# An encoder on one core: gather rows beside the projections paced at 0.42 and not 0.7, and taken in turn with leftover routing in the experts' pass

## The chip, the cores and the metric

The kernel runs on one core of one Trainium2 chip. The metric is the device time of one execution in microseconds (us), and the median over several executions counts. One execution was also profiled; every view below comes from it. PE is TensorE (matmuls), PEld its weight loads, DVE is VectorE, ACT is ScalarE, POOL is GpSimd, and SP is SyncE, which here only issues DMAs.

## The reference, cut to what matters

An encoder layer runs on two requests of 256 and 1024 tokens (ten tiles of 128 tokens) of width 1024. First come a mixer (retention and latent attention) and a cross attention over memory tokens. The last step, where most of the time goes, is a layer of 16384 single-neuron experts, of which each token uses 128:

```python
q = (xt @ wq).reshape(PEER_BLOCK, PEER_HEADS, PEER_QUERY_DIM)
s1 = jnp.einsum('thd,hkd->thk', q[..., :half], sub_keys[0])
s2 = jnp.einsum('thd,hkd->thk', q[..., half:], sub_keys[1])
v1, i1 = lax.top_k(s1, PEER_TOPK)
v2, i2 = lax.top_k(s2, PEER_TOPK)
...
ts, sel = lax.top_k(cand, PEER_TOPK)
ids = jnp.take_along_axis(cidx, sel, axis=-1).reshape(PEER_BLOCK, PEER_HEADS * PEER_TOPK)
g = jax.nn.softmax(ts.astype(jnp.float32), axis=-1).reshape(PEER_BLOCK, PEER_HEADS * PEER_TOPK)
a = jnp.einsum('td,ted->te', xt, U[ids]).astype(jnp.float32)
w = (g * jax.nn.gelu(a, approximate=False)).astype(xt.dtype)
return jnp.einsum('te,ted->td', w, V[ids])
```

Choosing the 128 experts of each token (the two lists of 16, their 16 best pairs, the ids and the weights g) is called routing below.

## The kernel before, in words

Matrix products are in float32, each made of three passes over split operands (`mm3`, L170: high times high, high times low, low times high).

The program has these stages. `phase_a` computes the retention. `phase_b` over block 0 (tiles 0 and 1) comes next, then `phase_m` for the second request (its latent attention, head pair by head pair), then `phase_b` over block 1 (tiles 2 to 5) and block 2 (tiles 6 to 9). A block in `phase_b` is a chain of projections: the output projection `w_out` with a residual add (`ld<-pj,ld`) and a norm, `ca_wq`, the cross attention, `ca_wo` with a residual add and a norm, and `peer_wq` with the key scores. Then `gates` (L1067) writes a table of gates, and `dense` (L1147) is the experts' pass.

The experts are computed in two ways. Six tiles (2 to 7) go through `dense`: for all 128 blocks of 128 experts, in 43 groups of three blocks (the last has two), PE computes the products with U (`pa`), ACT and DVE make the gated weights (`wr`, `wl`), and PE multiplies these with V (`pv`); DVE adds each result to the tile's sum (`dacc<-pv,dacc`, six per group). POOL makes the low halves of the weights U and V (`ul`, L1175, and `vl`, L1199). The other four tiles (0, 1, 8, 9: `GATHER`) fetch only the experts that their tokens chose. For each of the 128 experts of a token, a gather row is one indirect DMA on POOL's queue (128 rows of 4 KB, one for each token, into a tile `grow`) and one DVE instruction over 128x1024: 128 rows of U (`gj<-grow,...`, a dot product) and then 128 rows of V (a multiply-add into a sum). Four tiles make 1024 gather rows.

Where a gather row finds its second operand depends on when it starts. `banks` (L1046) copies x or the sum into PSUM (`gps`) if the pool `gps` exists, which is opened just ahead of `dense` (L1265). Before that the operand stands in SBUF (`gx`, `gacc`). The tiles `grow` rotate over four slots; `gx` and `gacc` join them when a tile starts after `gps` is open, and three more when all routing is done.

Routing and gather rows are generators in two queues, `self.routing` and `self.gathering`. They are laid beside the projections by a pace: as the program is written out, every matmul group calls `tick(us)` with its estimated time, `tick` adds `us * rho` to a debt, and `step` writes pieces of one queue until the debt is paid (a gather row counts 1.2). `RHO` (L50) has a pair for each stage, the first number for as long as routing waits in its queue, the second when only rows do: `phase_m` and `phase_b` of blocks 1 and 2, then `gates`, then `dense`. `step` takes routing first and rows only when no routing is left. What is left when `dense` has been written out is written behind it. A scheduler then puts each engine's instructions into a fixed order; each engine runs its own in that order and waits where an operand is late.

Of the kernel before, what the change touches and what calls it, by code (L numbers as in the profile page):

```python
# [46 lines left out]
NG = 3  # L47
O1_BY = "va"

RHO = ((0.75, 0.7), (0.5, 0.0), (0.9, 0.55))  # L50
LATE = 2

MORE = 3
# [10 lines left out]
class Lead:  # L64


    def __init__(self, k):
        self.k = k
# [39 lines left out]
class K:  # L108
    def __init__(self, nc, tc, I, O, dbg=None):
        self.nc, self.tc, self.I, self.O = nc, tc, I, O  # L110
        self.dbg = dbg or {}
        self.n = 0
        self.routing, self.gathering = [], []
        self.keeps = []
        self.spare = ()
        self.routed = set()
        self.owed, self.rho = 0.0, (0.0, 0.0)
        self.gps = self.rp = None
        self.slots, self.at = ["grow"] * 4, 0
        self.anchor = None  # L120
        self.v, self.vf = Lead(self), Fill(self)

    def tick(self, us):


        rho = self.rho[0 if self.routing else 1]
        if self.rho is RHO[1] and self.routed.issuperset(DENSE):
            rho = 0.0
# [5 lines left out]
            self.owed -= self.step()  # L134

    def step(self, q=None):
        q = q or self.routing or self.gathering
        try:
            return next(q[0])
        except StopIteration:  # L140
            q.pop(0)
            if self.gps is not None and not self.routing and self.rp is not None:

                self.rp.release()
                self.rp = None
                self.more = self.tc.alloc_tile_pool(name="more", bufs=1, side="right", reuse_waits="tile")
                self.slots += ["more"] * MORE
            return 0.0
# [1083 lines left out]
    def run(self):  # L1232
        nc, tc, I = self.nc, self.tc, self.I
        with ExitStack() as es:
# [21 lines left out]
            self.phase_b(sd, BLOCKS[:1], lambda: self.phase_m(sd, 0, self.lw))  # L1256
            self.rho = RHO[0]
            self.phase_m(sd, 1, self.lw)
            self.mw.release()
            self.phase_b(sd, BLOCKS[1:])  # L1260
            self.rho = RHO[1]
            self.dense_inputs(es.enter_context(tc.tile_pool(name="dx", bufs=1, reuse_waits="tile")))
            self.gates(sd)
            self.rho = RHO[2]
            self.gps = es.enter_context(tc.tile_pool(name="gps", bufs=1, reuse_waits="tile", space=PSUM))  # L1265
# [81 lines left out]
```

## Time and profile before

| | |
|---|---|
| median of three runs | 4372.47 us (4365.78 to 4373.7) |
| profiled execution, its own time | 4367.04 us |
| its span, first to last instruction | 4365.2 us |
| busy share of the span: PE, DVE, POOL, ACT | 92%, 75%, 53%, 38% |
| mean granted TensorE clock | 0.967 of full speed |

A busy PE is one with matmuls in its pipeline, and not a PE at its peak. What counts is which wait ends last in a stage, so the stages are read one by one: `phase_m` for the second request to about 1114 us, block 1 to 1490, block 2 to 1822, `gates` to 2111, `dense` to the end. Granted clock 1.00 is 2.4 GHz; a half-speed stretch is 1.2 GHz.

### The profile page before, as it was taken

Reading aid. Unit: us, or ns where it says so; the run is one execution under the profiler, and the core shown is the slowest. Engines: PE = TensorE matmul, PEld = TensorE weight load, DVE = VectorE, ACT = ScalarE, POOL = GpSimd, SP = SyncE. Lnnn points to the kernel's source line nnn. Section 1 sums busy time; section 2 is a strip of 40 time slices with the busy share of each in tenths; the row PEclk is TensorE's granted clock in tenths of the full one; section 3 lists DMA queues with packets and bytes.
Section 4 is the critical chain, followed back from the end, with each engine's and each line's share of the span. In section 5 each row is a group of like instructions: output and inputs, shape, how many; then the busy total and the mean of one; then the engine's idle time right before and its main releaser. Section 6 shows DMA issues by size and latency. Waiting matters only on the chain.

```text
span 4365.2 us, 66436 instructions
## 1 busy us (share of the span) xinstructions
PE 4010.5 (92%) x23202; PEld 3578.9 (82%) x23202; DVE 3281.7 (75%) x7044; ACT 1639.9 (38%) x3569; POOL 2301.6 (53%) x2090
## 2 busy tenths in 40 slices
PE   7999988899788988887798999999999999999999
PEld 7999877666587877876787888888988889888888
DVE  5556422798576799699788878888887888878883
ACT  6333535455343243498522222222222223222223
POOL 2221244013667710277537776666777677766662
PEclk9999999899899989999999999999999999999999
DMA  2112578237789866577648988888888889888882
GB/s 89 37 40 71 202 240 286 80 103 223 261 271 334 278 227 228 186 219 211 212 127 295 325 302 297 311 294 299 310 307 301 285 300 328 316 298 295 289 286 85
DMA packets 489008, 1030.74 MB, mean 236 GB/s; under 512 B 42720, under 2 KB 201952, under 8 KB 488672
## 3 DMA queue, kind: packets, MB, share of 16 engines
q0 software_dynamic: 149536, 545.33, 35.5%
q1 hardware_dynamic: 329200, 470.66, 32.6%
q10 hardware_dynamic: 9936, 10.51, 0.8%
q8 instruction: 182, 2.98, 0.3%
q14 instruction: 154, 1.26, 0.1%
HBM read 901.87 MB, written 124.45 MB: 235 GB/s over the span
## 4 chain that ended last, share of the span: by engine, by line
PE 26%; issue 8%; POOL 6%; DVE 6%; DMA 3%; ACT 1%; SPq 0%; POOLq 0%; ACTq 0%; DVEq 0%
PE pa L175 5%; PE pa L173 5%; PE pa L174 5%; PE pv L174 4%; PE pv L173 4%; PE pv L175 4%; POOL grow L1025 4%; DMA ur<-in_uT 2%; POOL vl L1199 1%; POOL ul L1175 1%; DVE gps L90 1%; DVE wr L74 1%; DVE dacc L74 1%; DVE wl L74 1%; DVE gj L90 1%
## 5 line engine op out<-in xcount | busy, mean ns | idle before, releaser
L1025 POOL DMA_INDIRECT grow<-in_peer_u,gids x512 | 537.1, 1049 | 533.9 <-DVE gj L90 213.0
L1025 POOL DMA_INDIRECT grow<-in_peer_v,gids x512 | 522.5, 1020 | 545.5 <-DVE gps L90 159.9
L173 PE MATMUL pa<-dxT,uh 128*128 128x384 f32 x2048 | 689.0, 337 | 17.4 <-ACT wr L1186 15.0
L174 PE MATMUL pa<-dxT,uh 128*128 128x384 f32 x2048 | 688.6, 336 | 0.0
L175 PE MATMUL pa<-dxT,ul 128*128 128x384 f32 x2048 | 676.4, 337 | 9.3 <-POOL ul L1175 9.3
L173 PE MATMUL pv<-vh,wh 128*128 128x512 f32 x1536 | 603.7, 397 | 40.1 <-DVE dacc L74 40.1
L174 PE MATMUL pv<-vl,wh 128*128 128x512 f32 x1536 | 609.7, 397 | 12.4 <-POOL vl L1199 11.7
L175 PE MATMUL pv<-vh,wl 128*128 128x512 f32 x1536 | 608.9, 396 | 1.4 <-DVE wl L74 1.4
L90 DVE SCALAR_TENSOR_TENSOR gps<-grow,ga,gps 128x1024 f32<-128x1024 f32 x384 | 493.2, 1284 | 9.6 <-ACT gps L1052 2.9
L90 DVE SCALAR_TENSOR_TENSOR gj<-grow,gps 128x1024 bf16<-128x1024 f32 x384 | 466.7, 1215 | 11.2 <-DMA grow<-in_peer_u,gids 3.1
L206 POOL TENSOR_TENSOR wl<-wraw,wh 128x512 fp32r<-128x512 f32 x180 | 250.7, 1409 | 310.7 <-ACT wh L202 241.2
L173 PEld LDWEIGHTS pa<-dxT,uh 128*128 128x128 f32 x2048 | 386.4, 189 | 31.7 <-ACT wr L1186 16.5
L1199 POOL TENSOR_TENSOR vl<-vr,vh 128x512 fp32r<-128x512 f32 x256 | 331.2, 1313 | 146.4 <-ACT vh L1198 144.3
L175 PEld LDWEIGHTS pa<-dxT,ul 128*128 128x128 f32 x2048 | 385.2, 189 | 21.2 <-POOL ul L1175 15.6
L1175 POOL TENSOR_TENSOR ul<-ur,uh 128x512 fp32r<-128x512 f32 x256 | 337.3, 1321 | 106.8 <-ACT uh L1174 103.5
L74 DVE TENSOR_TENSOR dacc<-pv,dacc 128x1024 f32<-128x1024 f32 x258 | 311.8, 1218 | 108.1 <-PE pv L175 107.6
L174 PEld LDWEIGHTS pa<-dxT,uh 128*128 128x128 f32 x2048 | 386.3, 189 | 6.3
L173 PEld LDWEIGHTS pv<-vh,wh 128*128 128x128 f32 x1536 | 292.7, 191 | 104.6 <-DVE dacc L74 48.5
L1174 ACT CAST uh<-ur 128x512 fp32r<-128x512 f32 x256 | 158.3, 621 | 553.4 <-DMA ur<-in_uT 510.2
L74 DVE TENSOR_TENSOR wr<-wr,gt 128x384 f32<-128x384 f32 x256 | 196.2, 767 | 209.2 <-ACT wr L1186 184.2
L174 PEld LDWEIGHTS pv<-vl,wh 128*128 128x128 f32 x1536 | 293.2, 191 | 73.2 <-POOL vl L1199 18.4
L175 PEld LDWEIGHTS pv<-vh,wl 128*128 128x128 f32 x1536 | 292.9, 191 | 58.4 <-DVE wl L74 1.8
(287 smaller groups left out, 9373.8 us busy)
## 6 DMA issues: line engine op xcount, KB each, us to landing
ur<-in_uT SPq DMA_DIRECT2D x256, 256.0 KB, 4.1
vr<-in_peer_v SPq DMA_DIRECT2D x256, 256.0 KB, 4.0
G<-st SPq DMA_DIRECT2D x96, 512.0 KB, 6.2
gt<-G SPq DMA_DIRECT2D x64, 768.0 KB, 7.2
wraw<-in_peer_wq SPq DMA_DIRECT2D x96, 256.0 KB, 5.9
wraw<-in_w_out SPq DMA_DIRECT2D x48, 256.0 KB, 5.1
wraw<-in_ca_wq SPq DMA_DIRECT2D x48, 256.0 KB, 3.6
x<-ld SPq DMA_DIRECT2D x24, 512.0 KB, 6.6
```

The costliest lines, as they stand in the source:

```text
L74: r = f(*a, **kw)
L90: r = f(*a, **kw)
L173: mm(ps, a[0], b[0], start=first, stop=False)
L174: mm(ps, a[0], b[1], start=False, stop=False)
L175: mm(ps, a[1], b[0], start=False, stop=last)
L206: (nc.vector if self.spare and k in self.spare else eng).tensor_tensor(wl[:, :n], raw[:, :n], r32(wh[:, :n]), ALU.subtract)
L1025: nc.gpsimd.indirect_dma_start(out=u, out_offset=None, in_=src, in_offset=bass.IndirectOffsetOnAxis(ap=ids[:, s:s + 1], axis=0))
L1174: nc.scalar.copy(uh, ur)
L1175: nc.gpsimd.tensor_tensor(ul, ur, r32(uh), ALU.subtract)
L1199: nc.gpsimd.tensor_tensor(vl, vr, r32(vh), ALU.subtract)
```

## The change

Two edits. The pace of gather rows beside `phase_m` and the blocks 1 and 2 falls from 0.7 to 0.42. And in `dense`, while both queues hold something, `step` takes a piece of routing and a gather row in turn.

```diff
-RHO = ((0.75, 0.7), (0.5, 0.0), (0.9, 0.55))
+RHO = ((0.75, 0.42), (0.5, 0.0), (0.9, 0.55))
...
+        self.turn = 0
...
     def step(self, q=None):
-        q = q or self.routing or self.gathering
+        if q is None:
+            q = self.routing or self.gathering
+            if self.rho is RHO[2] and self.gathering:
+
+                self.turn += 1
+                q = (self.gathering if self.turn % 2 else self.routing) or q
         try:
             return next(q[0])
```

The computation and the number of instructions of each kind stay. What moves is seen in the order of the instructions. In all of it, `gj` and `gacc` or `gps` mark gather rows of U and V, `ld`, `rs` and `act` belong to the projections.

On DVE, in block 1, around the residual adds behind `ca_wo`. Before:

```order
L74 TENSOR_TENSOR ld_14613<-pj_14669,ld_14613 128x512
L90 SCALAR_TENSOR_TENSOR gj_14185,ga_11155<-grow_14183,gx_11150 128x1024
L90 SCALAR_TENSOR_TENSOR gj_14223,ga_11155<-grow_14221,gx_11150 128x1024
L90 SCALAR_TENSOR_TENSOR gj_14258,ga_11155<-grow_14256,gx_11150 128x1024
L90 SCALAR_TENSOR_TENSOR gj_14299,ga_11155<-grow_14297,gx_11150 128x1024
L74 TENSOR_TENSOR ld_14615<-pj_14709,ld_14615 128x512
L90 SCALAR_TENSOR_TENSOR gj_14324,ga_11155<-grow_14322,gx_11150 128x1024
L90 SCALAR_TENSOR_TENSOR gj_14368,ga_11155<-grow_14366,gx_11150 128x1024
L90 SCALAR_TENSOR_TENSOR gj_14416,ga_11155<-grow_14414,gx_11150 128x1024
L74 TENSOR_TENSOR ld_14617<-pj_14744,ld_14617 128x512
```

On DVE at the same place, in the changed program:

```order
L74 TENSOR_TENSOR ld_14409<-pj_14465,ld_14409 128x512
L90 SCALAR_TENSOR_TENSOR gj_14508,ga_11155<-grow_14506,gx_11150 128x1024
L90 SCALAR_TENSOR_TENSOR gj_14524,ga_11155<-grow_14522,gx_11150 128x1024
L74 TENSOR_TENSOR ld_14411<-pj_14499,ld_14411 128x512
L90 SCALAR_TENSOR_TENSOR gj_14542,ga_11155<-grow_14540,gx_11150 128x1024
L90 SCALAR_TENSOR_TENSOR gj_14561,ga_11155<-grow_14559,gx_11150 128x1024
L74 TENSOR_TENSOR ld_14413<-pj_14533,ld_14413 128x512
```

Two rows stand between two adds where three or four stood. Counted on DVE's whole order, 41 gather rows and not 68 stand ahead of the first residual add of block 1, 115 and not 172 ahead of that of block 2, 115 and not 191 ahead of the first add behind block 2's `ca_wo`, and 130 and not 208 ahead of the first `wr` of `dense`. Of the 130, 128 are the U rows of tile 0, so its 128 V rows now all start after `gps` is open.

On DVE at the start of `dense` (`tv`, `ti`, `rs` are routing, `wr` and `wl` belong to the first group). Before:

```order
L74 TENSOR_TENSOR wr_24460<-wr_24460,gt_24397 128x384
L74 TENSOR_TENSOR wr_24509<-wr_24509,gt_24397 128x384
L74 TENSOR_TENSOR wl_24462<-wr_24460,wh_24461 128x384
L90 MAX tv_24415<-rs_24474 128x8 x3
L74 TENSOR_TENSOR wl_24511<-wr_24509,wh_24510 128x384
L90 MAX tv_24415<-rs_24474 128x8
```

The same place on DVE in the changed program:

```order
L90 SCALAR_TENSOR_TENSOR gps_24181<-grow_24211,ga_11155,gps_24181 128x1024
L74 TENSOR_TENSOR wr_24214<-wr_24214,gt_24149 128x384
L74 TENSOR_TENSOR wr_24259<-wr_24259,gt_24149 128x384
L74 TENSOR_TENSOR wl_24216<-wr_24214,wh_24215 128x384
L90 MAX tv_24196<-rs_24198 128x8
L90 SCALAR_TENSOR_TENSOR gps_24181<-grow_24242,ga_11155,gps_24181 128x1024
L90 MAX tv_24196<-rs_24198 128x8
L74 TENSOR_TENSOR wl_24261<-wr_24259,wh_24260 128x384
```

Rows of V into PSUM now stand between pieces of routing. Up to the last `dacc` of the fifth group, `dense` holds 84 gather rows on DVE and held 67; routing is the same.

On DVE at the end of the program (`fst` and the scaling of `dacc` by it are the final norm). Before, from the last sum on:

```order
L74 TENSOR_TENSOR dacc_24396<-pv_44236,dacc_24396 128x1024
L74 RECIPROCAL fst_44283<-fst_44283 128x1
L74 SCALAR_TENSOR_TENSOR dacc_24395<-dacc_24395,fst_44283,fw_44252 128x1024
L74 RECIPROCAL fst_44290<-fst_44290 128x1
L74 SCALAR_TENSOR_TENSOR dacc_24396<-dacc_24396,fst_44290,fw_44252 128x1024
```

The changed program's DVE, from the last sum on (five of the rows that follow it and the last three instructions):

```order
L74 TENSOR_TENSOR dacc_24148<-pv_44208,dacc_24148 128x1024
L90 SCALAR_TENSOR_TENSOR gps_41766<-grow_44144,ga_38901,gps_41766 128x1024
L74 SCALAR_TENSOR_TENSOR dacc_24146<-dacc_24146,fst_44251,fw_44227 128x1024
L74 RECIPROCAL fst_44258<-fst_44258 128x1
L90 SCALAR_TENSOR_TENSOR gps_41766<-grow_44158,ga_38901,gps_41766 128x1024
L74 SCALAR_TENSOR_TENSOR dacc_24147<-dacc_24147,fst_44258,fw_44227 128x1024
L90 SCALAR_TENSOR_TENSOR gps_41766<-grow_44175,ga_38901,gps_41766 128x1024
...
L90 SCALAR_TENSOR_TENSOR gps_41766<-grow_44289,ga_38901,gps_41766 128x1024
L74 RECIPROCAL fst_44296<-fst_44296 128x1
L74 SCALAR_TENSOR_TENSOR grow_44295<-gps_41766,fst_44296,grow_44292 128x1024
```

Twelve gather rows and three scalings stand behind the last `dacc`, where two scalings stood; seven more rows stand inside the last group, and the groups 41 and 42 hold 20 and 21 rows where they held 4 and none. On POOL the last three V splits stand behind fourteen row gathers.

## Rows read from the trace of the kernel before

**Rows 1.** Windows by stage: length, PE, PEld, DVE, ACT, POOL busy, clock, DMA, GB/s.

```profile
884.00:964.00 80.00, 73.59 (x434) 53.17 (x431) 72.77 (x269) 42.80 (x81) 9.02 (x9) 0.96 0.23 71
...
1040.00:1114.00 74.00, 69.55 (x434) 50.90 (x434) 64.10 (x126) 42.22 (x80) 29.38 (x28) 1.00 0.79 256
1114.00:1222.00 108.00, 80.79 (x384) 64.39 (x384) 65.05 (x96) 33.07 (x69) 72.61 (x57) 0.83 0.80 270
1222.00:1342.00 120.00, 105.68 (x669) 95.51 (x667) 89.00 (x152) 45.88 (x121) 85.96 (x68) 0.94 0.80 268
1342.00:1490.00 148.00, 132.50 (x988) 126.50 (x989) 97.22 (x171) 55.98 (x122) 105.03 (x79) 0.93 0.91 316
1490.00:1569.00 79.00, 58.99 (x269) 47.62 (x268) 76.06 (x219) 24.33 (x47) 35.17 (x32) 0.85 0.85 295
1569.00:1680.00 111.00, 102.77 (x688) 92.46 (x687) 103.54 (x533) 47.33 (x128) 2.81 (x3) 1.00 0.52 170
1680.00:1822.00 142.00, 130.09 (x982) 124.70 (x980) 109.60 (x453) 51.10 (x109) 18.15 (x17) 0.95 0.72 249
...
2111.00:2433.00 322.00, 287.07 (x1418) 255.26 (x1416) 266.80 (x650) 90.36 (x159) 173.35 (x136) 0.97 0.68 227
2433.00:4250.00 1817.00, 1771.29 (x8815) 1599.61 (x8815) 1498.32 (x1749) 472.96 (x863) 1275.51 (x1164) 0.99 0.86 302
4250.00:4300.00 50.00, 50.00 (x255) 45.60 (x255) 20.66 (x25) 17.11 (x29) 15.69 (x13) 1.00 0.33 104
```

**Rows 2.** The same, row gathers alone: length, POOL busy (count), clock, DMA, GB/s.

```profile
884.00:964.00 80.00, 9.02 (x9) 0.96 0.23 71
...
1040.00:1114.00 74.00, 29.38 (x28) 1.00 0.79 256
1114.00:1222.00 108.00, 33.04 (x27) 0.83 0.80 270
1222.00:1342.00 120.00, 51.06 (x44) 0.94 0.80 268
1342.00:1490.00 148.00, 47.78 (x39) 0.93 0.91 316
1490.00:1569.00 79.00, 22.13 (x22) 0.85 0.85 295
1569.00:1680.00 111.00, 2.81 (x3) 1.00 0.52 170
1680.00:1822.00 142.00, 18.15 (x17) 0.95 0.72 249
```

**Rows 3.** Waits of PE in block 1, longest first: total, times, longest.

```profile
PE tr L219 <- DVE ld L74: 11.5, 2, 5.8
```

**Rows 4.** Waits of DVE from 884 to 2111 us: total, times, longest.

```profile
DVE gj L90 <- DMA grow<-in_peer_u,gids: 29.9, 16, 4.8
DVE gacc L90 <- DMA grow<-in_peer_v,gids: 26.3, 12, 9.7
```

**Rows 5.** Gather rows on DVE, grouped: 1338-1790 us, 2111-2433 us (two), 2433-4250 us.

```profile
L90 DVE SCALAR_TENSOR_TENSOR gacc<-grow,ga,gacc 128x1024 f32<-128x1024 f32 x80 | 124.2, 1552 | 27.0 <-DMA grow<-in_peer_v,gids 26.3
...
L90 DVE SCALAR_TENSOR_TENSOR gacc<-grow,ga,gacc 128x1024 f32<-128x1024 f32 x48 | 69.6, 1449 | 5.7 <-DMA grow<-in_peer_v,gids 5.0
...
L90 DVE SCALAR_TENSOR_TENSOR gj<-grow,gps 128x1024 bf16<-128x1024 f32 x19 | 23.1, 1216 | 0.2
...
L90 DVE SCALAR_TENSOR_TENSOR gps<-grow,ga,gps 128x1024 f32<-128x1024 f32 x380 | 488.0, 1284 | 9.5 <-ACT gps L1052 2.9
```

**Rows 6.** Timeline of DVE near the end: start, length, instruction, [idle before].

```profile
4211.01 5.25 DVE L90 SCALAR_TENSOR_TENSOR gps<-grow,ga,gps 128x1024 f32<-128x1024 f32 x4
...
4340.88 1.23 DVE L74 TENSOR_TENSOR dacc<-pv,dacc 128x1024 f32<-128x1024 f32 x1 [2.86 <-PE pv L175]
...
4357.19 1.22 DVE L74 TENSOR_TENSOR dacc<-pv,dacc 128x1024 f32<-128x1024 f32 x1
...
4360.16 1.28 DVE L74 SCALAR_TENSOR_TENSOR dacc<-dacc,fst,fw 128x1024 f32<-128x1024 f32 x1
```

## The prediction

> **What bounds the kernel now.** I read the windows by stage first, then the same windows for the row gathers alone, then the waits of PE and DVE, the gather rows grouped by form, and the end of DVE's timeline. The windows show two regimes. In the experts' pass PE is all but full: 1771.29 of 1817 us at a granted clock of 0.99 between 2433 and 4250 us, and the chain of waits there runs over PE's own instructions for the most part. From 4250 us the rows are gone and PE is busy for 50.00 of 50 us [rows 1]. In blocks 1 and 2 PE is neither full nor at full clock: 80.79 of 108 us at a granted clock of 0.83 around block 1's `w_out`, 58.99 of 79 us at 0.85 around block 2's [rows 1]. There the stages are chains (matmul, residual add, norm, transposes, next matmul), and what ends last is often DVE: PE's largest wait in block 1 is 11.5 us for the residual and norm instructions [rows 3]. DVE itself stood still for 29.9 and 26.3 us behind gather rows whose data had not landed [rows 4], 56.2 us over the 208 rows that it runs ahead of the experts' pass; whatever stood behind such a row waited too.
>
> **What moves.** By the order, 208 gather rows ran ahead of the first `wr` and 130 do now, two of these belonging to the experts' pass already. So 80 rows leave the projections: 27 of them `phase_m` (68 against 41 ahead of block 1's first add), 10 block 1 up to `ca_wo`, 20 the rest of block 1, 19 the stretch from block 2's `w_out` to its `ca_wo`, four the rest. They come back in the experts' pass: 17 in its first five groups (84 against 67), 37 in groups 41 and 42, 19 in the last group and behind it, the rest between. Nothing else changes in number.
>
> **Gain beside the projections.** In `phase_m` a head pair took 80 us with 9 row gathers and 74 us with 28, at the same 434 matmuls [rows 1, 2]: rows are hidden there, and I set these 27 at nothing. Their cover is DVE's idle time, which `phase_m` has without them too; were it gone, they would cost what those in block 1 cost. For blocks 1 and 2 I compare equal work. Attention and `ca_wo` took 120 us in block 1 with 44 gathers and 111 us in block 2 with 3; `peer_wq` with its scores took 148 us with 39 and 142 us with 17 [rows 1, 2]. That is 15 us for 63 rows, 0.24 us each. It is no clean pair, since block 2 carries routing on DVE and takes low halves of weights from memory instead of making them on POOL, so it is an estimate. At 0.24 us the 34 rows outside the third stretch are worth 8 us. That stretch, 1490 to 1569 us, loses all its rows; PE idles 20.0 us in it and DVE is busy for 76.06 of 79 us [rows 1]. Routing moves up into their place, so I take half of the idle time, 10 us. Together 18 us. The bounds: nothing, if the chains would wait all the same, and above, PE's idle time and lost clock in proportion to the rows that go. Block 1 has 57.0 us idle and loses 36 us to the clock (0.17 of 108, 0.06 of 120, 0.07 of 148 us), and 30 of its 104 rows go: 27 us. The stretch in block 2 has 20.0 us and 0.15 of 79 us, 12 us, and all go: 32 us. So at most 59 us. I stay near the pair, because it compares whole stages; an idle time counts as the rows' only if they caused it.
>
> **The rows' own price.** A V row whose sum stands in SBUF took 1552 ns on average beside the projections (80 of them) and 1449 ns in the experts' pass (48); with the sum in PSUM it took 1284 ns (380) [rows 5]. Since all V rows of tile 0 now start with the sum in PSUM, DVE saves 80 times 268 ns and 48 times 165 ns, 29.3 us of busy time. The Trainium skill, page SBUF — State Buffer, section Who interferes with whom, says that a DVE instruction with two SBUF inputs contends with a GpSimd instruction that reads SBUF, and one with at most one such input does not. By that rule, the trace agrees: POOL makes low halves in both stretches, and only the rows with two SBUF inputs are stretched; were every stretched nanosecond on the path, the time would be that of the second rival below. In the sum the 21.4 us beside the projections are a part of the 18 us, not an addition; what more they could do is a rival.
>
> **Cost at the start of the experts' pass.** From 2111 to 2433 us DVE is busy for 266.8 of 322 us and PE for 287.07 [rows 1]. Of DVE's time 69.6 and 23.1 us are the 67 rows [rows 5]. Now 84 rows at 1284 ns make 107.9 us, 15.2 us more. Between nothing (DVE has 55 us idle) and 15 us (it runs `dacc` and `wl`, for which PE waits), I take half, 7 us: the stretch is fuller than any later one, but not full. Taking turns doesn't add work, it keeps the pace of 0.9 going for about twice as long.
>
> **Cost in groups 41 and 42.** A group of the full stretch took 1817 us over 35, 51.9 us, at 8815 matmuls over 35, 252. Without rows 255 matmuls took 50 us, so 252 take 49.4 us [rows 1]. Carrying about 21 rows thus costs a group 2.5 us. Two groups that had 4 and no rows carry 20 and 21: 5 us.
>
> **Cost at the end.** Before, the last `dacc` begins at 4357.19 us and the last scaling at 4360.16 us, 2.97 us later, and then only the output's DMA follows [rows 6]. Now twelve rows and three scalings stand between the last `dacc` and the norm of tile 9. Rows that add into one sum follow each other at 5.25 us for four, 1.31 us [rows 6]; twelve make 15.7 us, three scalings at 1.28 us 3.8 us, and the norm of tile 9 takes the place of the norm of the last dense tile. That is 19.5 us, and nothing hides it, since PE has finished. The last `dacc` itself moves too. In the last group, 16.3 us from 4340.88 to 4357.19 us [rows 6], seven rows, 9 us, come on top of five earlier adds and their scalings, which left about 5 us; one scaling goes behind. I take 3 us. The three V splits behind fourteen gathers on POOL can start only when DVE has freed the slots; the last products need them at once: 2 us, an estimate between nothing and three splits. Together 24 us, bounds 19 and 30.
>
> **Sum.** 4367.0 (the profiled execution's own time) - 18 + 7 + 5 + 24 = 4385 us. That execution lay 5.4 us below the median of the runs shown, so I put the forecast half that higher, at 4387 us. About 0.2% of the time, 8.7 us, is what a measurement of this kernel can tell from no change, so the band of no change is 4364 to 4381 us.
>
> **Rivals.** First, the rows hold up the projections by as much as the upper bound: 4385 - 41 = 4344, with the shift 4347 us, faster. The mechanism is DVE's order: a late row ahead of a residual add or a norm stops the chain, PE idles, and the granted clock falls to half speed behind the pause. The 56.2 us of waits for landings speak for it [rows 4]; `phase_m`, where rows cost nothing [rows 1, 2], against it. It decides when the gain passes 45 us, the 36 us of costs and the band. Second, the stretched V rows were on the path: then the gain is their 21.4 us and the 10 us of block 2's `w_out`, 31 us, and the start of the experts' pass gains 1 us where I charge 7: 4364, shifted 4367 us, no change. For it speaks that DVE is nearly full in that stretch; against it, that only some rows are long. Third, more slowly than forecast: at the start only four slots hold rows while routing lasts, and DVE waits for landings in the experts' pass as it did beside the projections, 56.2 us over 208 rows, 0.27 us each, for 84 rows 23 us and not 7: 4401, shifted 4404 us. Against it: the 48 rows there waited 5.0 us in all [rows 5]. That the change does nothing is excluded, since the counts in the order differ.
>
> **How the numbers follow.** The forecast has 0.45, within 4374 to 4400 us by its own terms, of which 0.06 falls into the band; the first rival 0.18, the second 0.22 (0.19 in the band and 0.03 below it, if block 1 gains as well), the third 0.15. So slower by over 0.2% has 0.54, no change 0.25, faster 0.21. The range, 4350 to 4408 us, leaves out half of the first rival and the upper part of the third, under 2 in 10.
>
> **What would show it.** Windows of the changed kernel: block 1 from its first `w_out` matmul to the last scores shorter than 372 us by some 5 to 10 us, block 2's `w_out` stretch shorter by about 10, `phase_m` unchanged; the first five groups 322 us or a little more; no `gacc` row; between the last `dacc` and the last scaling some 20 us more than 2.97. Wrong it would be above all if blocks 1 and 2 got shorter by over 30 us, with PE's granted clock there back near 0.95 or above, or if the first five groups took much longer than 330 us.

## The result and the profile after

The changed kernel takes 4350.01 us in the median of eight runs (4335.85 to 4359.02), the kernel before 4371.45 us beside it (eight runs, 4365.78 to 4377.08). The ratio is 0.9949, with an interval of 0.9934 to 0.9965: faster by half a per cent. The forecast was 4387 us, slower. The profiled execution of the changed kernel has a time of 4342.5 us and a span of 4340.7 us, 24.5 us under the span before.

Where the stages end was read off both traces at the start of the same instructions: a stage of the blocks begins and ends with PE's last key scores of the block ahead and its own, `phase_m` with the last product of its attention, a group of the experts' pass with its last `dacc`. The lengths, in us, of the profiled executions of both kernels and of those of the experiments below:

```
                   phase_m  block 1  block 2  gates  groups  groups  groups  group 43
                   ends at                           1-5     6-40    41-42   and end
before             1117.5   372.1    332.0    289.8  321.5   1817.1   90.9   24.3
after              1111.0   343.2    308.2    292.3  323.5   1819.1   96.5   46.9
e1 pace alone      1113.9   343.9    308.6    293.7  317.2   1835.7  102.1   79.6
e2 turns alone     1120.4   374.3    334.3    290.2  335.5   1826.9   90.8   24.4
e3 dense at 0.60   1111.3   348.2    306.9    290.7  324.4   1820.8   90.8   24.4
e4 no rows         1116.7   291.3    305.2    288.2  346.7   1913.4  103.8   24.4
e5 no gathers      1117.0   330.0    300.6    291.1  322.9   1820.5   90.9   24.3
e6 short rows      1108.9   336.8    327.3    292.1  323.2   1809.5   90.8   24.4
e7 V rows held     1118.1   356.0    315.5    287.2  323.7   1844.5   99.4   70.3
e8 0.33 and 0.60   1116.6   332.5    308.8    289.0  325.3   1845.8   91.6   24.4
e9 rows unread     1119.5   369.5    299.8    288.1  322.5   1805.7   90.8   24.4
e10 neither        1109.7   288.1    310.3    287.8  321.8   1821.6   90.9   24.3
```

So block 2 ends 59.2 us earlier (1762.4 against 1821.6 us): 6.5 us come from `phase_m`, 28.9 from block 1, 23.8 from block 2. Later stages give 34.7 us back: 2.5 in `gates`, 2.0 in groups 1 to 5, 2.0 in groups 6 to 40, 5.6 in groups 41 and 42, 22.6 in the last group and behind it. The gain repeats: e1 and e3 below run the changed program up to the experts' pass, and e2 the program of before. From PE's last key scores of block 0, ahead of every gather row, to those of block 2 the changed program takes 991.1, 991.9 and 996.5 us in these three executions, and the program of before 1050.5 and 1053.4.

Windows by stage of the changed kernel, in the columns of [rows 1], cut where its own stages end:

```profile
1035.00:1108.00 73.00, 70.34 (x439) 51.13 (x441) 53.28 (x104) 43.49 (x82) 19.12 (x19) 1.00 0.58 186
1108.00:1197.00 89.00, 70.83 (x331) 56.64 (x328) 51.64 (x69) 29.76 (x61) 61.51 (x48) 0.85 0.79 268
1197.00:1308.00 111.00, 103.37 (x701) 95.51 (x700) 76.06 (x137) 47.44 (x128) 69.12 (x54) 0.98 0.74 240
1308.00:1454.00 146.00, 133.19 (x1003) 126.72 (x1002) 78.17 (x192) 56.46 (x122) 91.19 (x73) 0.96 0.85 291
1454.00:1518.00 64.00, 55.56 (x276) 46.83 (x275) 59.19 (x244) 24.03 (x47) 9.76 (x8) 0.89 0.56 189
1518.00:1622.00 104.00, 99.53 (x685) 91.37 (x684) 96.75 (x505) 46.98 (x128) 0.00 (x0) 1.00 0.48 160
2055.00:2378.00 323.00, 288.47 (x1409) 257.52 (x1408) 283.68 (x661) 85.76 (x153) 177.44 (x154) 0.95 0.76 251
2378.00:4197.00 1819.00, 1769.95 (x8818) 1591.41 (x8817) 1495.82 (x1777) 477.31 (x870) 1280.31 (x1173) 0.99 0.86 305
```

The row gathers alone, in the columns of [rows 2]:

```profile
1108.00:1197.00 89.00, 24.41 (x18) 0.85 0.79 268
1197.00:1308.00 111.00, 37.64 (x30) 0.98 0.74 240
1308.00:1454.00 146.00, 35.58 (x30) 0.96 0.85 291
1454.00:1518.00 64.00, 0.00 (x0) 0.89 0.56 189
```

In block 1 the gathers fell from 110 [rows 2] to 78, and the granted clock of its second and third stretch rose from 0.94 and 0.93 [rows 1] to 0.98 and 0.96. Around its `w_out` PE is still idle for 18 of 89 us at 0.85. Block 2's `w_out` has no gather left and takes 64 us where it took 79. The first five groups show that DVE took more (283.68 us against 266.80 before) and that PE's stretch did not grow with it. The 35 groups behind them are as full as before.

The largest wait of DVE for rows, from 884 to 2055 us (total, times, longest), and the largest of PE in block 1:

```profile
DVE gj L90 <- DMA grow<-in_peer_u,gids: 16.2, 8, 6.5
```

```profile
PE tr L225 <- DVE act L74: 9.1, 7, 2.8
PE tr L225 <- DVE ld L74: 6.4, 1, 6.4
```

Waits for landings fell from 56.2 us [rows 4] to 16.2, and the wait of the transposes for the residual add from 11.5 us [rows 3] to 6.4; the one for `act` is 9.1 us and was 8.0. On the profile page's list of costliest groups all 512 V rows stand in one form, at 1283 ns (ACT copies tile 0's sum into PSUM for it, with two copies that the kernel before did not have):

```profile
L90 DVE SCALAR_TENSOR_TENSOR gps<-grow,ga,gps 128x1024 f32<-128x1024 f32 x512 | 657.0, 1283 | 9.3 <-DMA grow<-in_peer_v,gids 1.5
```

The timeline of DVE at the end, which answers to [rows 6]:

```profile
4313.68 1.20 DVE L74 TENSOR_TENSOR dacc<-pv,dacc 128x1024 f32<-128x1024 f32 x1
...
4323.35 10.56 DVE L90 SCALAR_TENSOR_TENSOR gps<-grow,ga,gps 128x1024 f32<-128x1024 f32 x8
4335.41 0.16 DVE L74 RECIPROCAL fst<-fst 128x1 f32<-128x1 f32 x1 [1.51 <-ACT fst L186]
4335.61 1.28 DVE L74 SCALAR_TENSOR_TENSOR grow<-gps,fst,grow 128x1024 f32<-128x1024 f32 x1
```

From the last `dacc` to the last scaling it is 21.93 us where it was 2.97: twelve rows and the scalings between them, as the order said, with nothing of PE beside them.

### The profile page after: what moved, and what is told of

Its sections match the earlier page's. It is cut to its first block, busy times and chain, and to the rows that moved or that the text cites. A ratio compares the mean times of both kernels' runs of the same rounds, so it can differ in the third digit from the quotient of the medians.

```text
span 4340.7 us, 66469 instructions
## 1 busy us (share of the span) xinstructions
PE 3994.5 (92%) x23202; PEld 3566.9 (82%) x23202; DVE 3264.3 (75%) x7044; ACT 1638.3 (38%) x3568; POOL 2267.5 (52%) x2090
## 4 chain that ended last, share of the span: by engine, by line
PE 24%; DVE 10%; issue 8%; DMA 5%; POOL 4%; ACT 1%; SPq 0%; POOLq 0%; DVEq 0%; ACTq 0%
PE pa L179 4%; PE pa L180 4%; PE pa L181 4%; PE pv L179 4%; PE pv L180 4%; PE pv L181 4%; DVE gps L90 3%; DMA ur<-in_uT 3%; POOL grow L1031 2%; DVE wr L74 2%; DVE dacc L74 2%; DVE gj L90 1%; DVE wl L74 1%; POOL vl L1205 1%; POOL ul L1181 1%
## 5 line engine op out<-in xcount | busy, mean ns | idle before, releaser
L1031 POOL DMA_INDIRECT grow<-in_peer_v,gids x512 | 510.7, 997 | 346.9 <-DVE gps L90 203.7
L90 DVE SCALAR_TENSOR_TENSOR gps<-grow,ga,gps 128x1024 f32<-128x1024 f32 x512 | 657.0, 1283 | 9.3 <-DMA grow<-in_peer_v,gids 1.5
L212 POOL TENSOR_TENSOR wl<-wraw,wh 128x512 fp32r<-128x512 f32 x180 | 239.9, 1351 | 339.4 <-ACT wh L208 254.9
```

The lines of the kernel that those rows point to most:

```text
L90: r = f(*a, **kw)
L212: (nc.vector if self.spare and k in self.spare else eng).tensor_tensor(wl[:, :n], raw[:, :n], r32(wh[:, :n]), ALU.subtract)
L1031: nc.gpsimd.indirect_dma_start(out=u, out_offset=None, in_=src, in_offset=bass.IndirectOffsetOnAxis(ap=ids[:, s:s + 1], axis=0))
```

## The experiments

**Each edit alone (e1, e2).** e1 is the kernel before with the pace alone:

```diff
-RHO = ((0.75, 0.7), (0.5, 0.0), (0.9, 0.55))
+RHO = ((0.75, 0.42), (0.5, 0.0), (0.9, 0.55))
```

> Only the pace is changed, 0.42 for 0.7; in the experts' pass routing stays ahead of rows. By the order 127 rows stand ahead of the first wr (208 before), and 37 behind the last dacc (12 in the changed kernel). Theory A, the rows beside the projections were dear (about 60 us for the 80 that left) and the turns matter little: the last scores of block 2 at about 1762 us as in the changed kernel, the end 25 more rows at 1.31 us later than there, 33 us, so about 4380 us, near the kernel before. Theory B, the gain comes from the turns (rows of the first groups with their sum in PSUM, routing spread): block 2 ends near 1822 us as before, and the time is over 4420 us.

It took 4395.79 us against 4372.98, ratio 1.0047 (1.0032 to 1.0062): slower, and some 16 us over the 4380 of theory A. Block 2 ends at 1766.4 us, so the gain beside the projections belongs to the pace and is all there. It is lost for the most part at the end, where 37 rows stand behind the last `dacc`: the last group and the end take some 55 us more than before, groups 41 and 42 11.2, groups 6 to 40 18.6. DVE's timeline there:

```profile
4334.52 1.21 DVE L74 TENSOR_TENSOR dacc<-pv,dacc 128x1024 f32<-128x1024 f32 x1
...
4344.19 43.69 DVE L90 SCALAR_TENSOR_TENSOR gps<-grow,ga,gps 128x1024 f32<-128x1024 f32 x33
...
4389.58 1.28 DVE L74 SCALAR_TENSOR_TENSOR grow<-gps,fst,grow 128x1024 f32<-128x1024 f32 x1
```

e2 is the changed kernel with the old pace, so with the turns alone:

```diff
-RHO = ((0.75, 0.42), (0.5, 0.0), (0.9, 0.55))
+RHO = ((0.75, 0.7), (0.5, 0.0), (0.9, 0.55))
```

> Only the turns; the pace beside the projections stays at 0.7, 211 rows ahead of the first wr, none behind the last dacc. Theory A: block 2 ends at 1822 us as before, the first five groups cost up to 15 us more or less, the time is 4360 to 4385 us, within 0.3% of the kernel before. Theory B: the time falls to about 4350 us, as with both edits.

It took 4399.12 us against 4372.98, ratio 1.0062 (1.0049 to 1.0075): slower too, and above both expectations. Blocks 1 and 2 stay as before (block 2 ends at 1829.0 us; 4.5 of the 7.4 us more stand already at the end of block 0, ahead of all rows), the first five groups take 14.0 us more, and groups 6 to 40 9.8 us more. Each edit by itself costs some 23 to 26 us, both together gain 21: the turns bring rows forward (to the end of the tenth group 329 rows have run in the changed kernel and 304 in e1), which leaves twelve at the end and not 37. With nothing left over at the end they have nothing to win there, and in e2 the first five groups carry 82 rows and not 67, 46 of them with two operands in SBUF. That this is what makes these groups longer is likely, but was not tried by itself.

**The end taken away (e3).** The changed kernel with a faster pace in the experts' pass:

```diff
-RHO = ((0.75, 0.42), (0.5, 0.0), (0.9, 0.55))
+RHO = ((0.75, 0.42), (0.5, 0.0), (0.9, 0.6))
```

> The changed kernel with a pace of 0.6 and not 0.55 for rows in the experts' pass: by the order the rows end one group before the last, none behind the last dacc. Theory A with the cost at the end as forecast (23 us, measured as 4 in the last group and 19 behind it): the end of the span 2 to 8 us behind the last dacc, the time about 20 us below the changed kernel, 4330 us. Rival: the denser rows slow the groups (DVE fuller by 4%) by 0.5 us and more each, and take the 20 us back: 4350 us.

It took 4329.13 us against 4372.98, ratio 0.9903 (0.9889 to 0.9916), with e8 the shortest of those that leave nothing out. All rows are done by the end of group 40, and the end is as it was before the change. DVE's timeline there, and the window of groups 6 to 40:

```profile
4309.46 1.23 DVE L74 TENSOR_TENSOR dacc<-pv,dacc 128x1024 f32<-128x1024 f32 x1
...
4312.43 1.29 DVE L74 SCALAR_TENSOR_TENSOR dacc<-dacc,fst,fw 128x1024 f32<-128x1024 f32 x1
```

```profile
2381.00:4202.00 1821.00, 1768.59 (x8817) 1588.14 (x8816) 1561.21 (x1839) 478.89 (x875) 1334.95 (x1226) 0.99 0.89 321
```

Groups 6 to 40 carry 810 rows here and 750 in the changed kernel, and take 1.7 us more: in these two executions 60 more rows were all but free there.

**No rows beside the projections (e4).** The changed kernel with a pace of nothing there, and a faster one in the experts' pass so that the rows come to an end:

```diff
-RHO = ((0.75, 0.42), (0.5, 0.0), (0.9, 0.55))
+RHO = ((0.75, 0.0), (0.5, 0.0), (0.9, 0.66))
```

> No gather rows beside the projections at all (pace 0), turns, and a pace of 0.66 in the experts' pass, so that the rows end in the last group. 10 rows stand ahead of the first wr. If each row beside the projections costs the same 0.75 us (60 us for 80), the 120 that still run there in the changed kernel are worth 90 us more, block 2 ends near 1670 us, and the time is about 4300 us with 15 us for 120 more rows in the experts' pass. If the price grows with density (rows cost only where they stand thick ahead of a chain), block 2 ends at 1740 to 1760 us and the time is 4330 to 4350 us.

It took 4386.11 us against 4372.98, ratio 1.0028 (1.0017 to 1.0039), more than either expectation, since the experts' pass pays for the rows: against the changed kernel the first five groups take 23.2 us more and groups 6 to 40 94.3. Up to the end of block 2 it is the control that the prediction lacked. Its windows of block 1 (`w_out`; attention to the first add behind `ca_wo`; the rest), of block 2's attention to its first add, and of groups 6 to 40:

```profile
1117.00:1180.00 63.00, 60.06 (x306) 49.74 (x306) 18.09 (x37) 29.52 (x62) 33.37 (x26) 0.97 0.62 204
1180.00:1252.00 72.00, 71.70 (x572) 69.99 (x571) 27.93 (x72) 41.21 (x118) 20.33 (x16) 1.00 0.36 117
1252.00:1408.00 156.00, 153.82 (x1123) 145.11 (x1122) 38.06 (x142) 60.59 (x130) 65.86 (x53) 1.00 0.58 183
...
1473.00:1551.00 78.00, 74.34 (x575) 70.74 (x574) 73.05 (x349) 42.09 (x119) 0.00 (x0) 1.00 0.45 154
...
2348.00:4261.00 1913.00, 1798.00 (x8778) 1599.32 (x8777) 1690.47 (x1950) 460.16 (x865) 1429.85 (x1314) 0.98 0.92 329
```

Ten rows run ahead of the experts' pass here, next to none of them in block 1. Without them block 1 takes 291.3 us and not 372.1, with PE busy for 285.58 of 291 us at full clock but for its first stretch. So the idle time and the lost clock there (93 us in the prediction's working), which it took as an upper bound, were for the most part the rows': 80.8 us went with them. Block 2 ends 49.2 us earlier than in the changed kernel for 120 rows fewer ahead of the experts' pass, 0.41 us each; the 78 rows between the kernel before and the changed one were worth 59.2 us there, 0.76 us each. These two rates mix places: 38 of the 120 rows stood in `phase_m`, which is no shorter without them (see the terms below). In block 1 alone, 73 rows cost 51.9 us, 0.71 each, and the 30 more of the kernel before 28.9 us, 0.96 each: the price of a row grows with their density, but less than 0.41 and 0.76 say. In the experts' pass density counts too: groups 6 to 40 carry 892 rows, 82 more than in e3, and take 92.6 us more, far outside the spread of all other kernels there (1805.7 to 1845.8 us).

**What a row costs with (e5, e6, e9, e10).** A gather row is a transfer and a DVE instruction. These four are the kernel before with one of them or both taken away ahead of the experts' pass. e5 issues no gathers there; e6 keeps them and lets DVE work on 8 of 1024 columns; e9 issues the gathers and lets DVE read data that has long been in SBUF; e10 has neither. The values of tile 0 are left out by this. The edits of e5, of e6 and of e9 (e10 has the first two):

```diff
         def rows(src, s):
+            if self.gps is None:
+                return fw
             u = row()
```

```diff
-            v.scalar_tensor_tensor(junk, u, 1.0, x3, ALU.mult, ALU.mult, accum_out=a[:, s:s + 1])
+            n = 8 if self.gps is None else D
+            v.scalar_tensor_tensor(junk[:, :n], u[:, :n], 1.0, x3[:, :n], ALU.mult, ALU.mult, accum_out=a[:, s:s + 1])
```

```diff
-            return u
+            return x3 if self.gps is None else u
```

> The kernel before, but the rows that run ahead of the experts' pass fetch nothing: their DVE instructions (208, same number and place) read one resident tile, and the 208 row gathers on POOL and their 109 MB fall away; the values of tile 0 are left out. Theory C, the rows are dear because of DVE's order and time: only the 56 us of landing waits can go, and those partly; the last scores of block 2 at 1790 to 1815 us (1822 before, 1762 changed). Theory D, they are dear because their traffic and their places on POOL's queue hold back the weights: 1715 to 1750 us, near the 1713 us without rows. The experts' pass as before.

> The kernel before, but ahead of the experts' pass the DVE instruction of a gather row works on 8 of 1024 columns (values of tile 0 left out); the gathers, their traffic and the waits for their landing stay. Theory C: DVE is free for the chains, the last scores of block 2 at 1720 to 1760 us. Theory D: 1800 to 1822 us. If both hold in part, this and the run without DMA each show a part, and the parts may add up to more than the 108 us that the run without rows gained.

> The kernel of before, with all gathers of rows issued, but ahead of the experts' pass the row instructions on DVE read the activations that are already in SBUF in place of the gathered row, so that no DVE instruction waits for a landing and no gather waits for DVE to free a slot (the values of tile 0's gathered rows are left out of the output). Theory L, the landing waits in DVE's order are what the transfers cost: block 2 ends near 1748 us as with no gathers at all, and the time is near 4300 us. Theory T, what the transfers cost is their traffic and POOL's time at the gathers, ahead of the weights' low halves: block 2 ends above 1790 us, and the time is 4340 us or more. In between, both.

> The kernel of before, with neither gathers nor full DVE instructions for rows ahead of the experts' pass (they work on 8 of 1024 columns of a resident tile; tile 0's values are left out of the output). If the rows' transfers and their DVE time are all that rows cost, block 2 ends where it did with no rows at all, 1713 us, and the time is near 4374 - 108 = 4266 us. If their places in the order cost something by themselves (208 instructions, and routing pushed back behind them), block 2 ends later, between 1725 and 1747 us, and the time is 4278 to 4300 us.

Measured: e5 4298.59 us, ratio 0.9828 (0.9811 to 0.9844); e6 4328.52, ratio 0.99 (0.9883 to 0.9916); e9 4322.18, ratio 0.9888 (0.9871 to 0.9904); e10 4263.83, ratio 0.9757 (0.974 to 0.9773). Block 2 ends at 1747.6, 1773.0, 1788.8 and 1708.1 us. So in the kernel before, transfers and DVE time together cost 113.5 us (1821.6 - 1708.1), about what e4 gave by moving the rows (108.4). DVE's time alone costs 39.5 us (e5 - e10), the transfers alone 64.9 us (e6 - e10). Both hold, and they nearly add up (104.4). The medians of the whole times, each against the kernel before beside it, say the same: 33 and 63 us. Windows of block 1, cut as for e4, of the kernel before, of e10, of e5 and of e6:

```profile
1117.00:1216.00 99.00, 72.35 (x315) 56.89 (x310) 57.12 (x78) 30.77 (x64) 67.02 (x53) 0.81 0.80 273
1216.00:1305.00 89.00, 77.58 (x567) 73.89 (x567) 69.92 (x133) 40.94 (x116) 59.95 (x47) 0.92 0.78 262
```

```profile
1110.00:1173.00 63.00, 59.91 (x305) 49.57 (x305) 29.64 (x90) 29.37 (x61) 33.38 (x26) 0.97 0.61 204
1173.00:1245.00 72.00, 71.81 (x572) 69.96 (x571) 36.66 (x149) 42.75 (x120) 20.22 (x16) 1.00 0.38 125
```

```profile
1117.00:1193.00 76.00, 63.07 (x307) 51.19 (x305) 62.19 (x90) 29.92 (x61) 47.56 (x26) 0.91 0.52 174
1193.00:1277.00 84.00, 76.68 (x571) 72.95 (x570) 74.79 (x145) 42.49 (x120) 29.48 (x16) 0.96 0.30 97
```

```profile
1109.00:1197.00 88.00, 69.97 (x305) 55.21 (x304) 29.79 (x82) 29.53 (x61) 56.55 (x52) 0.84 0.86 306
1197.00:1273.00 76.00, 72.86 (x573) 69.81 (x572) 40.49 (x131) 41.57 (x118) 50.23 (x48) 1.00 0.90 315
```

Around `w_out` (63 us in e10) the transfers cost most: 88 us in e6, at a clock of 0.84 though DVE is busy for a third of it, against 76 in e5. In the attention (72 us in e10) DVE's time costs most, 84 us in e5 against 76 in e6. Without DVE's work e6 still waits for landings, DVE from 1114 to 1822 us:

```profile
DVE gacc L90 <- DMA grow<-in_peer_v,gids: 52.6, 24, 8.6
DVE gj L90 <- DMA grow<-in_peer_u,gids: 25.8, 14, 4.3
```

A second path is the weights. PE's waits for their high halves, which ACT makes, from 1114 to 1822 us in the kernel before, in e6 and in e10:

```profile
PE pj L173 <- ACT wh L202: 14.3, 5, 8.2
```

```profile
PE pj L173 <- ACT wh L202: 12.5, 4, 6.0
```

```profile
PE pj L173 <- ACT wh L202: 2.1, 2, 1.2
```

Behind it stands ACT's own wait for the weights of block 1's `w_out` to land: 32.1 us before and 32.8 in e6, 14.1 in e5 and 14.5 in e10. So beside the gathers the weights come later to where they are needed.

e9 asks whether the waits for landings are the transfers' whole price. They are not: it gains 32.8 us at block 2's end, less than half of e5's 74.0. Nearly all of it is in block 2 (299.8 us against 332.0), and block 1 is hardly shorter than before (369.5 us). There POOL's gathers, which no longer wait for DVE, crowd into the first stretch: the row gathers in it, and PE's longest wait of that stretch:

```profile
1119.00:1235.00 116.00, 50.08 (x45) 0.79 0.93 335
```

```profile
PE pj L174 <- POOL wl L206: 34.7, 7, 30.5
```

44 gathers begin there (the line counts one more that reaches into it) and 21 by the same cut in the kernel before, and a low half of a weight that POOL makes comes 30.5 us late. POOL's timeline shows why: in those 30.5 us it runs 14 gathers and the four loads of `act` ahead of that subtraction, one after the other, and several of the gathers wait for an earlier one to land in their slot. So the time fell between both theories: the wait for landings is one part, POOL's queue and the weights that come later the other, and taking the wait away by itself moves the bunch to where POOL is needed. No run separates POOL's time at the gathers from their traffic.

**Number or density (e7).** The kernel before at 0.7, but with tile 0's V rows held until the experts' pass, so that about as few rows run ahead of it as in the changed kernel (134 against 130), as densely as before:

```diff
+        if self.rho is RHO[0] and not self.routing and self.held:
+            rho = 0.0
...
+            self.held = s == P - 1 and not banked
```

> The kernel before with the pace of 0.7, but tile 0's V rows are held back until the experts' pass: 134 rows stand ahead of the first wr, as in the changed kernel, at the density of the kernel before until they are used up in block 1's peer_wq (68, 115 and 131 ahead of block 1's two first adds and block 2's); routing first in the experts' pass. If a row's price is its own, wherever it stands, block 2 ends 56 to 60 us earlier, at 1762 to 1768 us. If density makes the price, phase_m and block 1 up to ca_wo gain nothing (first ca_wo add at 1305 us) and block 2 ends at 1775 to 1790 us. Behind the last dacc some 30 rows, as with the pace alone.

It took 4413.87 us against 4374.16, ratio 1.009 (1.007 to 1.0111). Block 1 reaches its first add behind `ca_wo` at 1305.4 us, where the kernel before has 1305.3 and the changed one 1279.5; block 2 ends at 1789.6 us. So about the same number of rows ahead of the pass is worth 32.0 us when the late ones go and 59.2 us when all are spread thinner: it is where they stand, not their number alone. Block 1 shows it at one place: 68 rows in 356.0 us, against 76 in 343.2 in the changed kernel; over e4's 291.3 us that is 1.00 us a row at the old density and 0.71 at the new one. What e7 loses is the end, with 30 rows behind the last `dacc` (the last group and the end take some 46 us more than before), groups 41 and 42 (8.5 us) and groups 6 to 40 (27.4 us, not explained).

**Thinner still (e8).** The changed kernel with 0.33 and 0.6:

```diff
-RHO = ((0.75, 0.42), (0.5, 0.0), (0.9, 0.55))
+RHO = ((0.75, 0.33), (0.5, 0.0), (0.9, 0.6))
```

> Both edits with a pace of 0.33 beside the projections and 0.6 in the experts' pass: 103 rows ahead of the first wr (130 in the changed kernel), the rows end in the last group but one. If the price between 0 and 0.42 is even (49 us for 120 rows, 0.41 us each), block 2 ends 11 us earlier than with 0.42, at 1752 us, the 27 more rows in the experts' pass cost 3 to 7 us, and the time is 4320 to 4326 us, below the 4329 us of 0.42 with 0.6. If the last rows that leave were nearly free, 4330 to 4335 us.

It took 4332.71 us against 4374.16, ratio 0.9903 (0.9886 to 0.9919), the same as e3 and not the 4320 to 4326 us hoped for. Block 2 ends 8.5 us earlier than in e3 and groups 6 to 40 take 25.0 us more in the profiled executions; the medians differ by 3.6 us. The paces 0.33 and 0.42 can't be told apart here.

## Why the prediction was wrong

**The step that failed** is the gain beside the projections: 18 us forecast, 59.2 measured, as much as the upper bound of 59 us that the prediction had worked out and set aside. The rate of 0.24 us per row, from the pair of block 1 and block 2, was wrong by a factor of three to four, for the pair was no control: the 34 rows that it was applied to gave 37.1 us and not 8, 1.09 us each, and e4 gives 0.71 for those that stay in block 1. The sign that the prediction named for its failure, blocks 1 and 2 shorter by over 30 us, is there with 52.7; the clock that it named with it came back in part (0.98 and 0.96 in block 1 behind `w_out`, 0.85 and 0.89 around the two `w_out`). e4 shows why the pair misled. From the start of the attention to the last scores block 1 took 274.1 us before and 228.4 without rows, so its rows cost 45.7 us. Block 2 took 252.7 us with its 20 gathers and 240.1 in e4 with three: it is 11.7 us longer than block 1 even so, and its own rows cost 12.6. The difference between the blocks, 21.4 us by these cuts (15 by the windows of the prediction), hides both.

What makes block 2 longer by itself was not isolated. One candidate is routing, which stands there behind the rows. From the attention to the first add behind `ca_wo` block 2 took 87 us with 3 gathers before, and takes 78 now. Its window before and after:

```profile
1569.00:1656.00 87.00, 78.77 (x582) 72.60 (x581) 79.74 (x384) 42.14 (x119) 2.81 (x3) 1.00 0.49 163
```

```profile
1518.00:1596.00 78.00, 73.53 (x570) 69.84 (x569) 72.52 (x348) 41.80 (x119) 0.00 (x0) 1.00 0.46 152
```

DVE ran 384 instructions there and now 348, and 32 of the 36 are routing, which rows further ahead had pushed back into it. e5, e9 and e4 fit, with 78, 78 and 77 us at 346 to 349 instructions. But e10 takes 81.8 us at 352, and e7 88.5 us with no gathers in it and 350 DVE instructions, at a clock of 0.94. So it is not shown that routing made the 9 us.

**The choice between pair and bound** rested on the sentence that an idle time counts as the rows' only if they caused it. They had, for the most part: without rows PE is busy for 285.58 of block 1's 291 us. The rate also left out the stretch that had no partner, block 1's `w_out`, where the rows cost 35 us (98 us from the end of `phase_m` to the attention before, with 21 gathers, and 63 in e4 with none).

**By terms**: of the 59.2 us block 1 gives 28.9 (forecast 7 of the 30 rows at 0.24 us), block 2's `w_out` with the few us ahead of it 15.6 (forecast 10), the rest of block 2 8.2 (forecast 1), `phase_m` 6.5 (forecast nothing). In `phase_m` some 5 us are the rows': from the last key scores of block 0, ahead of every row, to its end it takes 344.8 to 346.4 us in the three kernels with all their rows at 0.7 (before, e2, e7), 339.3 to 341.4 in the three at 0.42 (after, e1, e3), and 341.0 in e4 with one row. So the 39 rows that stay there are hidden, as the prediction said, and the 24 that left were not quite.

**The costs were right**: groups 1 to 5 +2.0 us (forecast 7, between 0 and 15), groups 41 and 42 +5.6 (forecast 5), the last group and the end +22.6 (forecast 24, between 19 and 30), together 30.2 against 36; `gates` and groups 6 to 40 add 4.5 (forecast nothing), no more than executions differ by. e3 and e1 confirm the end's mechanism: with no row behind the last `dacc` it is gone, with 37 it grows to 60.1 us of the span.

**The rivals.** The first, faster at 4347 us, came true in its time. That the gain equals its bound is in part luck: block 1 gives 28.9 us where the bound had 27, block 2 23.8 where it had 32, and `phase_m` 6.5 where it had nothing. Its mechanism, late rows in DVE's order, is one part of the cause: with the waits for landings taken away e9 gains 32.8 us, nearly all in block 2. e6 does not speak against it, since it keeps those waits (78.4 us, the two lines of DVE in e6 above). What the rival left out is that the rows also load POOL and the DMA engines, from which the weights come.

The second rival held that only the stretched V rows were on the path. The stretch itself is real, and the trace of the kernel before shows where it comes from: of the 80 V rows beside the projections, the 27 that overlap one of POOL's subtractions take 2096 ns and the 53 others 1275 ns. With the sum in PSUM no V row is longer than 1292 ns, though 178 of 384 overlap a subtraction. The Trainium skill, page SBUF — State Buffer, section Who interferes with whom, says that a DVE instruction with two SBUF inputs contends with a GpSimd instruction that reads SBUF. By that rule, the trace agrees. In e5, with no gathers in flight, the rows with two SBUF inputs still take 1500 ns, so it isn't the gathers that stretch them. But 21.4 us of stretch could not explain 59.2. The third, waits for landings in the experts' pass, did not come: the first five groups are 323.5 us long, not 344. That e2 takes 335.5 there shows that it was not far off at another density.

**What stays open**: groups 6 to 40 take 1805.7 to 1821.6 us in six kernels with about the same rows there (before, after, e5, e6, e9, e10), and 9.8 us more than before in e2, 18.6 in e1, 27.4 in e7, 28.7 in e8. The number of rows in them doesn't explain it (741 in e1 and 744 in e7 against 745 before; 822 in e8 and 810 in e3, 25.0 us apart), and no run was made for it. Runs of one kernel differ by up to 23 us (the changed one), so that single executions say little about 10 us there. Open too is how the 64.9 us of the transfers divide between waits for landings, POOL's time and the traffic, which meet in one chain.

## What to carry to other kernels

Work laid beside a chain as filler has a price that depends on where it stands and grows with its density (here nothing for the last 39 rows in `phase_m`, 0.71 to 1.00 us in block 1); one rate per piece, from two unlike stages that both carry some of it, understated it by a factor of three or more. Take the filler away in one run before pricing it: the idle time and the lost clock of the stage that vanish with it are its price. And filler that is spread thinner must come out somewhere: here 22.6 of the 59.2 us were paid back in the last group and behind it, and a little more pace in the full stage (0.6 and not 0.55) took most of that back.

## What the runs showed of the hardware that was not expected

The transfers of the rows cost the projections more than DVE's instructions on them, 64.9 against 39.5 us. The mean of a row instruction on 8 of 1024 columns is far from 128 times shorter. The V rows of blocks 1 and 2, grouped, in e5 (all columns, no gathers), in e6 (8 columns, beside gathers) and in e10 (8 columns, no gathers), with busy time, mean ns and idle time before:

```profile
L90 DVE SCALAR_TENSOR_TENSOR gacc<-grow,ga,gacc 128x1024 f32<-128x1024 f32 x80 | 120.0, 1500 | 1.2
```

```profile
L90 DVE SCALAR_TENSOR_TENSOR gacc<-grow,ga,gacc 128x8 f32<-128x8 f32 x80 | 37.8, 473 | 53.3 <-DMA grow<-in_peer_v,gids 52.6 <-DVE gacc L90 0.3
```

```profile
L90 DVE SCALAR_TENSOR_TENSOR gacc<-grow,ga,gacc 128x8 f32<-128x8 f32 x80 | 22.5, 281 | 1.9
```

On 8 columns the mean is 281 ns without gathers and 473 ns beside them, on all columns 1500 ns. It is not the gathers that lengthen it. The traces tell the instructions that overlap one of POOL's subtractions from the others. On 8 columns the others take 224 ns in e10 (73 of 80) and 219 ns in e6 (65), so the gathers make no difference to them; those that overlap take 872 ns (7) and 1573 ns (15). On all columns in e5 it is 1278 ns (50) against 1870 ns (30). So a short instruction with two SBUF operands is not safe from POOL: the longest on 8 columns took 4.3 us.
